# Keys of the dilated groups, and group 0's values, turned in 32x32 blocks and moved through DRAM instead of being transposed on TensorE

## The chip, the cores and the metric

The kernel runs on one core of a Trainium2 chip. The metric is the device time of one execution in microseconds (us). The runs of the kernel before took 853.75 to 854.53 us, with a median of 854.29 us.

## The reference, cut to what matters

The reference computes two layers on 512 tokens of 1024 channels, with 16 heads of 64. Layer A is the one that is changed. It projects the normalised tokens to queries, keys and values of three dilated groups (dilations 1, 4 and 16) and to a gate, and attends in each group to a window of neighbours:

```python
for g, (window, dilation) in enumerate(DILATED_PAIRS):      # (128, 1), (512, 4), (2048, 16)
    q = rms_norm(qkv[:, :, g, 0], q_gain[g])
    k = rms_norm(qkv[:, :, g, 1], k_gain[g])
    v = qkv[:, :, g, 2]
    reach = (window // 2) // dilation
    o, lse = dilated_group_attention(q, k, v, t5_bias[...], dilation, reach)
    outs.append(o)
    lses.append(lse)
alpha = jax.nn.softmax(jnp.stack(lses), axis=0)
y = jnp.sum(alpha[..., None] * jnp.stack(outs), axis=0)
y = y.reshape(b, s, BRANCH_WIDTH) * jax.nn.silu(gate)
return y @ w_out
```

Layer B, neighbourhood attention on an 8 x 64 grid, is not changed. All data are float32. A large product is made on TensorE as three products of a high and a low part (`wh`, `wl`, `hn_h`, `hn_l`).

## The kernel before, in words

**Pairs.** Layer A goes through eight pairs of heads, `hc` = 0 to 7; the text calls them the first to the eighth pair. For each pair `main_a(hc)` makes the large products: first 512 columns with the keys and values of groups 1 and 2 (`rawk`), then 512 columns with three queries and group 0's key (`rawq`), then 128 columns of group 0's values (`v0_a`), then 128 of the gate. A tile of weights is 512 columns of `wraw`; ScalarE (ACT) casts it to `wh`, VectorE (DVE) or GpSimd (POOL) subtracts to get `wl` (`split`, L127 and L131). There are four buffers of `wh` and of `wl`, and three of `wraw`, each with two tiles. A tile feeds twelve products of TensorE (PE).

**Attention beside it.** `side` yields the attention of the pair before in small pieces between the products. `scores(u)` makes the scores of half of the tokens (u = 0 and 1) into `log`, `softmax` makes `p`, and `turner` turns `p` in 32x32 blocks on DVE into `tr`, writes that to DRAM (`td`, L736) and reads it back in four parts (`pt`, L740). `weigh` multiplies `pt` with the values into `o`. Queries and group 0's key of the first six pairs are moved in the same way: `turn_q` turns `rawq`, `move_q` writes `qd` (L578) and reads `qt` (L584), and `split_q` makes `k0h`, `q0h`, `k0l`, `q0l` of it, which the next `scores` needs.

**Keys before.** `k_a(hc)` takes `rawk`, makes two sets of four 128x128 transposes on PE into PSUM (`transpose4`, tile `tp`, L210), and DVE multiplies each set with the gains into `k12` (L527). **Values before.** `v0_a` scales and permutes group 0's values into `vt` (L504), POOL copies 64 columns to its head (L505), and `v_a` makes one set of four transposes and an ACT copy into `v0` (L615).

**What sets the order.** PE's order is the order of the code. `clock` adds up a modelled time of the products; `side` goes on when `clock` has reached a due time, and `later_on(delay, job)` runs a job when `clock` has passed. Every DMA of the loop is issued by SP, in one order; an instruction there that waits holds up all behind it, the weight loads (L175) included. The order on DVE, ACT and POOL is a scheduler's, except where an instruction is kept in program order. Each pair's bias tiles `e` are read by six small DMAs (L690, L695). In the third pair `bias_rows` adds the loads and stores of `rp`, `gb_d` and `lb_d` for layer B.

Of the kernel before, what the change touches and what calls it, by code (L numbers as in the profile page):

```python
# [13 lines left out]
F32 = mybir.dt.float32  # L14
# [8 lines left out]
P = 128  # L23
# [19 lines left out]
def tile_hybrid_encoder(  # L43
# [222 lines left out]
    def squares(v, ss, i, ns):  # L266
        sq = wk.tile([P, 512], F32, tag="sq", name="sq")[:, : ns * 64]
        if len(v.shape) == 3:
            v = v.rearrange("p (a f) r -> p a f r", f=4)
            nc.gpsimd.tensor_mul(sq.rearrange("p (f a r) -> p a f r", f=4, a=4), v, v)  # L270
        else:
# [7 lines left out]
    def head_norm(raw, ss, ns, held, delay=0):  # L279


        rs = wk.tile([P, 32], F32, tag="rs", name="rs")
        rsqrt(nc.vector if ns == 8 else nc.gpsimd, rs[:, : 4 * ns], ss[:, : 4 * ns], 4 * ns, 1.0 / DH)

        def scale():
            for i in range(4):
                by = rs[:, i * ns : (i + 1) * ns].unsqueeze(2)
                if len(raw.shape) == 4:
                    v = raw[:, :, i, :].rearrange("p (h a f) r -> p f h a r", h=2, f=4)
                    by = rs[:, i * ns : (i + 1) * ns].rearrange("p (f h) -> p f h", h=2)  # L290
                    by = by.unsqueeze(3).unsqueeze(4).to_broadcast([P, 4, 2, 2, 32])
                else:
                    v = raw[:, i, : ns * 64].rearrange("p (a b) -> p a b", b=64)
                    by = by.to_broadcast([P, ns, 64])
                m = nc.vector.tensor_mul(v, v, by)
                if held or delay:
                    tc.keep_in_program_order(m)

        if held:
            later.append(scale)  # L300
        elif delay:
            later_on(delay, scale)
        else:
            scale()
# [15 lines left out]
    def trj(t):  # L320
        return t.rearrange("p (s j) -> p s j", j=4)
# [3 lines left out]

    ng = cp.tile([P, 2, KT], F32, name="ng")
    rs_n = cp.tile([P, 4], F32, name="rs_n")
    rs_trj = cp.tile([P, S], F32, name="rs_trj")
    rs_half = cp.tile([P, S], F32, name="rs_half")

    def spread():
# [38 lines left out]
    def scales_a():  # L370
        pa = spread()
        nc.scalar.mul(tjr(rs_half), to_tjr(pa), 0.5)
        nc.scalar.copy(trj(rs_trj), to_trj(pa))

    def norm(layer, k, xk):

# [45 lines left out]

    moved = lambda hc: hc < NHC - 2

    def part(n):
        return rk[:, 1024 * n : 1024 * n + 1024].rearrange("p (i c) -> p i c", i=4)

    def project_qk(n, ns, key, hc, guard, first=False, **kw):

        box = []  # L430

        def evac(i, acc):
            if not box:
                if key == "rawq":
                    t = wk.tile([P, 4 * n], F32, tag="rawq", name=key, bufs=1)
                    box.append(
                        t.rearrange("p (c i r) -> p c i r", c=16, i=4)
                        if moved(hc)
                        else t.rearrange("p (i c) -> p i c", i=4)
                    )  # L440
                elif key == "rawk":
                    box.append(part(0))
                    st["v12", hc] = part(1 + hc % 3)
# [12 lines left out]
            for dst, src in pieces:  # L456
                if first:
                    nc.scalar.copy(dst, src)
                else:
                    nc.scalar.activation(dst, src, AF.Copy, scale=rs_n[:, i : i + 1])  # L460
            if not first:
                squares(raw[:, :, i, :] if key == "rawq" and moved(hc) else raw[:, i, : ns * 64], ss, i, ns)

        tile_of = lambda hn: lambda k, i: hn[:, k, P * i : P * (i + 1)]
        yield from project(tile_of(hn_h), tile_of(hn_l), n, evac, guard, **kw)
        raw, ss = box
        if first:
            st["first"] = raw, ss
            return
        normed(raw, ss, ns, key, hc)  # L470

    def normed(raw, ss, ns, key, hc):
        head_norm(raw, ss, ns, key == "raw", 9000 if key == "rawk" and 0 < hc < NHC - 1 else 0)
        if key == "rawq" and moved(hc):
            turn_q(raw)
        st[key, hc] = raw
        stamp[key, hc] = clock[0]

    def first_out():

        raw, ss = st.pop("first")
        for i in range(4):
            for t in (raw, st["v12", 0]):
                nc.scalar.activation(t[:, i, :], t[:, i, :], AF.Copy, scale=rs_n[:, i : i + 1])
            squares(raw[:, i, :], ss, i, 4)
        normed(raw, ss, 4, "rawk", 0)

    def gate_a(hc):
# [10 lines left out]
    def v0_a(hc):  # L499
        acc = []  # L500
        yield from project_t(acc)
        yield "v", hc - 1
        vt = wk.tile([P, EXT], F32, tag="vt", name="vt", bufs=1)
        nc.vector.tensor_mul(trj(vt[:, 64:EXT]), to_trj(acc[0]), trj(rs_trj))  # L504
        nc.gpsimd.tensor_copy(vt[:, 0:64], vt[:, EXT - 64 : EXT])  # L505
        st["vt", hc] = vt
        stamp["vt", hc] = clock[0]

# [10 lines left out]
            yield from gate_a(hc)  # L519

    def k_a(hc):
        yield "wait", ("rawk", hc), 12500 if hc == 0 else 22500 if hc < NHC - 1 else 10000
        k12 = wk.tile([P, 2, 512], F32, tag="k12", name="k12", bufs=1)
        raw = st.pop(("rawk", hc))
        for g in range(2):
            tp = transpose4(raw, g * P)
            nc.vector.tensor_scalar(k12[:, g, :], tp, gk[:, g + 1 : g + 2], None, op0=ALU.mult)  # L527
# [80 lines left out]
    def v_a(hc):  # L608

        yield "wait", ("vt", hc), 2500  # L610
        vt = st.pop(("vt", hc))
        tp = bank("tp")
        for i in range(4):
            transpose(tp[:, i * P : (i + 1) * P], vt[:, i * P : (i + 1) * P])
        nc.scalar.copy(v0[hc % 2], tp.rearrange("p (i c) -> p i c", i=4))  # L615
        stamp["v", hc] = 0
        yield

# [127 lines left out]
    def attn_a(hc):  # L746
# [7 lines left out]
        def scores(u):  # L754
# [94 lines left out]
        if hc < NHC - 1:  # L849
            for u in range(2):  # L850
# [285 lines left out]
    def side():  # L1136
# [19 lines left out]
        stamp["rs", "a"] = 0  # L1156
        for hc in range(NHC):
            if hc < NHC - 1:
                yield from k_a(hc)
                yield from chain(q_a(hc), v_a(hc))  # L1160
                if moved(hc):
                    yield from st.pop(("land", hc))
                yield from attn_a(hc)
# [114 lines left out]
```

## Time and profile before

| | |
|---|---|
| median of the runs | 854.29 us |
| the profiled execution, whole | 854.65 us |
| its span, first to last instruction | 852.7 us |
| PE busy | 843.6 us (99%) |
| DVE, ACT, POOL busy | 520.2, 431.3, 307.1 us |
| DMA on SP's queue | 140.24 MB, 53.7% of 16 engines |
| TensorE clock granted | full speed in all slices of the span |

PE's busy time overlaps from one product to the next, so a busy PE may still have small gaps: they are read from the chain of waits, which lists stretches of one line with their start and length. A window's DMA share is the mean busy share of the 16 DMA engines in that stretch. A group's row gives the count, then the busy time in us and the mean length of one in ns, then the idle time ahead and what ended it.

### The profile page before, as it was taken

What the parts mean: (1) busy time and instruction counts of PE and PEld (TensorE: products, weight loads), DVE (VectorE), ACT (ScalarE), POOL (GpSimd) and SP (SyncE); (2) the same over time, 40 slices, a digit from 0 to 9 for tenths busy, and PEclk for the clock granted to TensorE, in tenths of its full rate; (3) what the DMA queues carried; (4) which work ended last, traced back from release to release, by engine and by line L of the source; (5) the groups of instructions that cost most, each with busy time, mean ns of one, the idle gap of its engine ahead of it and who ended that gap; (6) DMA issues with size and microseconds to landing.
All of it is one profiled execution on the core that took longest, in us unless ns stands there. A gap on an engine that the chain in (4) does not pass through costs nothing.

```text
span 852.7 us, 15400 instructions
## 1 busy us (share of the span) xinstructions
PE 843.6 (99%) x5547; PEld 702.7 (82%) x5547; DVE 520.2 (61%) x1335; ACT 431.3 (51%) x924; POOL 307.1 (36%) x493
## 2 busy tenths in 40 slices
PE   8999999999999999999999999999999999999998
PEld 6788878788788788788788787789998898889786
DVE  6445684674675675675675745447567656766642
ACT  7433653653652652652653554355366655665531
POOL 2252541542542542542531341121344335542411
PEclk9999999999999999999999999999999999999999
DMA  7346277477478378378375562174245654555223
GB/s 250 111 130 208 87 226 219 153 222 227 137 230 241 105 239 240 98 238 238 96 247 153 147 190 78 60 244 142 82 142 150 168 162 149 170 163 160 99 98 126
DMA packets 65372, 141.23 MB, mean 166 GB/s; under 512 B 5904, under 2 KB 23248, under 8 KB 65296
## 3 DMA queue, kind: packets, MB, share of 16 engines
q1 hardware_dynamic: 65008, 140.24, 53.7%
q8 instruction: 44, 0.72, 0.4%
q14 instruction: 32, 0.26, 0.1%
q10 hardware_dynamic: 288, 0.01, 0.0%
HBM read 109.11 MB, written 31.12 MB: 164 GB/s over the span
## 4 chain that ended last, share of the span: by engine, by line
PE 87%; ACT 4%; DMA 4%; DVE 3%; issue 1%; POOL 1%; SPq 0%; ACTq 0%; POOLq 0%; DVEq 0%
PE acc L206 74%; PE log L206 5%; PE o L206 5%; PE tp L210 3%; DMA qd<-rawq 1%; ACT p L655 1%; ACT p L814 1%; DMA rp<-in_rpb 1%; ACT p L1067 1%; DMA qt<-qd 1%; POOL sq L270 1%; ACT wh L127 1%; DMA hg<-in_head_gain 0%; DVE wl L131 0%; DMA eb<-lb_d 0%
## 5 line engine op out<-in xcount | busy, mean ns | idle before, releaser
L127 ACT CAST wh<-wraw 128x512 fp32r<-128x512 f32 (+1 forms) x276 | 162.0, 588 | 291.4 <-PE acc L206 251.0
L206 PE MATMUL acc<-wh,hn_h 128*128 128x512 f32 (+1 forms) x768 | 294.2, 383 | 1.7 <-ACT wh L127 0.9
L206 PE MATMUL acc<-wh,hn_l 128*128 128x512 f32 (+1 forms) x768 | 286.3, 373 | 0.0
L206 PE MATMUL acc<-wl,hn_h 128*128 128x512 f32 (+1 forms) x768 | 285.8, 372 | 0.4 <-DVE wl L131 0.4
L131 POOL TENSOR_TENSOR wl<-wraw,wh 128x512 fp32r<-128x512 f32 (+1 forms) x110 | 137.0, 1245 | 359.4 <-ACT wh L127 320.0
L131 DVE TENSOR_TENSOR wl<-wraw,wh 128x512 fp32r<-128x512 f32 (+1 forms) x166 | 111.1, 670 | 135.8 <-ACT wh L127 131.5
L206 PEld LDWEIGHTS acc<-wh,hn_h 128*128 128x128 f32 x768 | 144.6, 188 | 29.3 <-issue 4.9
L206 PEld LDWEIGHTS acc<-wh,hn_l 128*128 128x128 f32 x768 | 144.4, 188 | 20.8
L206 PEld LDWEIGHTS acc<-wl,hn_h 128*128 128x128 f32 x768 | 144.8, 189 | 19.8 <-DVE wl L131 0.9
L206 PE MATMUL acc<-hn_h,wh 128*128 128x512 f32 x192 | 77.0, 401 | 0.9 <-ACT rawq L460 0.6
L206 PE MATMUL acc<-hn_h,wl 128*128 128x512 f32 x192 | 74.9, 390 | 0.0
L206 PE MATMUL acc<-hn_l,wh 128*128 128x512 f32 x192 | 74.8, 390 | 0.0
L655 ACT ACTIVATE p<-p,mn 128x512 f32<-128x512 f32 (+3 forms) x128 | 69.3, 586 | 0.0
L814 ACT ACTIVATE p<-p,mn 128x512 f32<-128x512 f32 (+1 forms) x64 | 44.8, 701 | 45.0 <-DVE mn L803 44.1
L273 DVE TENSOR_REDUCE ss<-sq 128x4 f32<-128x256 f32 (+1 forms) x96 | 48.4, 504 | 30.7 <-POOL sq L272 19.7
L727 DVE STREAM_TRANSPOSE tr<-p 128x512 f32<-128x512 f32 (+1 forms) x80 | 53.7, 682 | 9.9 <-ACT p L655 9.5
L272 POOL TENSOR_TENSOR sq<-rawk 128x256 f32<-128x256 f32 x64 | 40.5, 639 | 52.7 <-ACT rawk L460 44.9
L206 PE MATMUL acc<-y_h,wh 128*128 128x512 f32 x128 | 52.1, 407 | 0.0
L206 PE MATMUL acc<-y_h,wl 128*128 128x512 f32 x128 | 50.0, 391 | 0.0
L206 PE MATMUL acc<-y_l,wh 128*128 128x512 f32 x128 | 49.9, 390 | 0.0
L206 PEld LDWEIGHTS acc<-hn_h,wh 128*128 128x128 f32 x192 | 36.1, 188 | 10.8 <-ACT rawk L460 2.1
L206 PEld LDWEIGHTS acc<-hn_h,wl 128*128 128x128 f32 x192 | 36.0, 188 | 7.7
(138 smaller groups left out, 1087.0 us busy)
## 6 DMA issues: line engine op xcount, KB each, us to landing
wraw<-in_w SPq DMA_DIRECT2D x95, 512.0 KB
wraw<-in_w SPq DMA_DIRECT2D x38, 384.0 KB
td<-tr SPq DMA_DIRECT2D x14, 1024.0 KB
pt<-td SPq DMA_DIRECT2D x56, 256.0 KB
qd<-rawq SPq DMA_DIRECT2D x6, 1024.0 KB
qt<-qd SPq DMA_DIRECT2D x24, 256.0 KB
td<-tr SPq DMA_DIRECT2D x6, 896.0 KB
pt<-td SPq DMA_DIRECT2D x24, 224.0 KB
```

The costliest lines, as they stand in the source:

```text
L127: nc.scalar.copy(h, raw)
L131: eng.tensor_sub(l, raw, h.bitcast(F32))
L206: nc.tensor.matmul(o, l, r, **kw)
L210: nc.tensor.transpose(o, i, ident)
L270: nc.gpsimd.tensor_mul(sq.rearrange("p (f a r) -> p a f r", f=4, a=4), v, v)
L272: nc.gpsimd.tensor_mul(sq, v, v)
L273: nc.vector.tensor_reduce(ss[:, i * ns : (i + 1) * ns], sq.rearrange("p (a b) -> p a b", b=64), axis=AX.X, op=ALU.add)
L655: nc.scalar.activation(pr, pr, AF.Copy, scale=mn[:, 3:4])
L727: nc.vector.transpose(dst, src[:, :n].rearrange("p (i b k) -> p i b k", b=4, k=32))
L814: nc.scalar.activation(row, row, AF.Exp, bias=mn[:, 1:2], scale=-1.0, accum_out=mn[:, 2:3])
L1067: nc.scalar.activation(pr[:, o : o + n], pr[:, o : o + n], AF.Exp, bias=mn[:, 0:1], scale=-1.0, accum_out=mn[:, 2:3])
```

## The change

The keys of the first seven pairs no longer pass PE's transposes. The evacuation of `rawk` writes them to a new layout (`rk_a`: four blocks `a` of 384 columns, of which the first 256 are the keys). After the scaling with the norm, DVE turns both groups in 32x32 blocks in place. `move_k` then writes the tile to DRAM in one DMA (`kd`) and reads it back as `k12` in four DMAs. The values of group 0 of the first six pairs are turned by DVE too, into the last 128 columns of each block, after POOL's copy; they travel with the keys of the next pair, and POOL then puts them into `v0`, doubled because they are now scaled with `rs_half` (`rs_trj` is gone). ACT multiplies `k12` with the gains in place. `attn_a` reads `k12` in four runs of 32 columns where it read 128 columns in a row. The first half's reads of `pt` are due 10500 instead of 8500 behind their write.

The place is shown on three engines. On PE, in the steady part (fifth pair), the keys' two sets of transposes stood between products of the next pair's projection (`acc` is the accumulator, `rawk` the keys); before:

```order
L206 MATMUL acc<-wh,hn_l 128x512
L210 MATMUL tp<-ident,rawk 128x128 x4
L206 MATMUL acc<-wh,hn_h 128x512
L206 MATMUL acc<-wl,hn_h 128x512
L206 MATMUL acc<-wh,hn_l 128x512
L206 MATMUL acc<-wh,hn_h 128x512
L206 MATMUL acc<-wl,hn_h 128x512
L206 MATMUL acc<-wh,hn_l 128x512
L210 MATMUL tp<-ident,rawk 128x128 x4
```

and after:

```order
L206 MATMUL acc<-wh,hn_l 128x512
L206 MATMUL acc<-wh,hn_h 128x512
L206 MATMUL acc<-wl,hn_h 128x512
L206 MATMUL acc<-wh,hn_l 128x512
L206 MATMUL acc<-wh,hn_h 128x512
L206 MATMUL acc<-wl,hn_h 128x512
L206 MATMUL acc<-wh,hn_l 128x512
L206 MATMUL acc<-wh,hn_h 128x512
```

The products follow each other without the transposes; over the program PE has 20 such sets less, 14 of keys and 6 of values.

On SP, in the third pair (`td` and `pt` are the turned scores, `rp`, `gb_d`, `lb_d` the bias of layer B, `e` the bias of the next pair), before:

```order
L736 DMA td<-tr 128x4x512
L411 DMA rp<-in_rpb 128x248
L175 DMA wraw<-in_w 128x1024
L740 DMA pt<-td 32x4x512 x2
L416 DMA gb_d<-rp 128x248
L417 DMA lb_d<-lb 128x376
L690 DMA e_2052<-l_d 128x1x256 x2
L695 DMA e_2053<-l_d 128x1x224 x4
L175 DMA wraw<-in_w 128x1024
L740 DMA pt<-td 32x4x512 x2
L736 DMA td<-tr 128x4x512
L175 DMA wraw<-in_w 128x1024
```

and after, from `lb_d` on (`k_1881` is `k12`):

```order
L424 DMA lb_d<-lb 128x376
L579 DMA kd<-rawk 128x4x384
L763 DMA e_2036<-l_d 128x1x256 x2
L768 DMA e_2037<-l_d 128x1x224 x3
L587 DMA k_1881<-kd 32x4x384 x4
L768 DMA e_2037<-l_d 128x1x224
L175 DMA wraw<-in_w 128x1024
L813 DMA pt<-td 32x4x512 x2
L809 DMA td<-tr 128x4x512
L813 DMA pt<-td 32x4x512 x3
L175 DMA wraw<-in_w 128x1024
```

The write of the keys and its four reads come in ahead of the first of these weight loads. Two reads of the first `td` that stood ahead of `gb_d` now stand behind the second `td`, and the first read of the second `td` has come ahead of the second weight load. In the other pairs the weight load behind the second `td` stands ahead of that read.

On DVE, in the fourth pair, before:

```order
L295 TENSOR_TENSOR rawk<-rawk,rs 128x256 x4
L131 TENSOR_TENSOR wl<-wraw,wh 128x512
```

and after:

```order
L301 TENSOR_TENSOR rawk<-rawk,rs 128x2x4x32 x4
L306 STREAM_TRANSPOSE rawk<-rawk 128x4x128 x2
L131 TENSOR_TENSOR wl<-wraw,wh 128x512
```

The two turns have come between the scaling and the next `wl`.

The diff, cut to its core:

```diff
@@ head_norm, scale()
+                elif len(raw.shape) == 5:
+                    v = raw[:, :, :, i, :].rearrange("p (h f) g x -> p g h f x", f=2)
+                    by = rs[:, i * ns : (i + 1) * ns].rearrange("p (g h) -> p g h", h=2)
+                    by = by.unsqueeze(3).unsqueeze(4).to_broadcast([P, 2, 2, 2, 32])
...
+            if len(raw.shape) == 5:
+                for g in range(2):
+                    tc.keep_in_program_order(nc.vector.transpose(raw[:, :, g, :, :], raw[:, :, g, :, :]))
...
@@ scales_a
-        nc.scalar.copy(trj(rs_trj), to_trj(pa))
...
+    moved_k = lambda hc: hc < NHC - 1
+    rk_a = rk[:, :1536].rearrange("p (a y) -> p a y", a=4)
...
@@ project_qk, evac
-                pieces = [(raw[:, i, :], acc[:, :256]), (st["v12", hc][:, i, :], acc[:, 256:])]
+                keys = raw[:, i, :], acc[:, :256]
+                if moved_k(hc):
+                    keys = raw[:, :, :, i, :], acc[:, :256].rearrange("p (g a x) -> p a g x", g=2, a=4)
+                pieces = [keys, (st["v12", hc][:, i, :], acc[:, 256:])]
...
@@ normed
+        if key == "rawk" and moved_k(hc):
+            move_k(hc, 17500 if hc else 4000)
...
@@ v0_a
-        nc.vector.tensor_mul(trj(vt[:, 64:EXT]), to_trj(acc[0]), trj(rs_trj))
+        in_trj = lambda t, order: t.rearrange(f"p ({order}) -> p t r j", t=4, j=4)
+        nc.vector.tensor_mul(
+            in_trj(vt[:, 64:EXT], "t r j"), in_trj(acc[0], "j t r"), in_trj(rs_half, "t j r")
+        )
         nc.gpsimd.tensor_copy(vt[:, 0:64], vt[:, EXT - 64 : EXT])
+        if moved(hc):
+            src = vt[:, :S].rearrange("p (i b x) -> p i b x", i=4, b=4)
+            dst = rk_a[:, :, 256:].rearrange("p b (i x) -> p i b x", i=4)
+            tc.keep_in_program_order(nc.vector.transpose(dst, src))
+            stamp["v", hc] = 0
+            return
...
+    def move_k(hc, delay):
+        n = 384 if hc else 256
+        d = dr.tile([4, P, 384], F32, name="kd", tag="kd", bufs=2)
+        box = []
+        def write():
+            tc.keep_in_program_order(nc.sync.dma_start(d.rearrange("a p y -> p a y")[:, :, :n], rk_a[:, :, :n]))
+            stamp["k12", hc] = 0
+        def read(a):
+            if not box:
+                box.append(wk.tile([P, 4, 384], F32, tag="k12", name="k12", bufs=1))
+            dst = box[0][32 * a : 32 * a + 32, :, :n]
+            src = d[a].rearrange("(b k) y -> k b y", b=4)[:, :, :n]
+            tc.keep_in_program_order(nc.sync.dma_start(dst, src))
+        def landed():
+            kv = box[0]
+            for g in range(2):
+                k = kv[:, :, P * g : P * g + P]
+                tc.keep_in_program_order(nc.scalar.activation(k, k, AF.Copy, scale=gk[:, g + 1 : g + 2]))
+            if hc:
+                src = kv[:, :, 256:].rearrange("p b (i x) -> p b i x", i=4)
+                dst = v0[(hc - 1) % 2].rearrange("p i (b x) -> p b i x", b=4)
+                nc.gpsimd.tensor_scalar(dst, src, 2.0, None, op0=ALU.mult)
+            st["k12", hc] = kv, st.pop(("v12", hc))
+        later_on(delay, write)
+        for n_, a in enumerate((0, 2, 1, 3)):
+            later_on(delay + 6000, partial(read, a))
+        later_on(delay + 17000, landed)
...
@@ attn_a
-                                k12[hs, g, P * j : P * j + P],
+                                sb(k12[hs], P * g + 32 * j, [[384, 4], [1, 32]]),
...
-                send = partial(turned.send, pq[:, 2048 * u : 2048 * u + 2048], 8500, 1200)
+                send = partial(turned.send, pq[:, 2048 * u : 2048 * u + 2048], 8500 if u else 10500, 1200)
...
@@ side
-                yield from k_a(hc)
-                yield from chain(q_a(hc), v_a(hc))
+                yield from q_a(hc)
                 if moved(hc):
                     yield from st.pop(("land", hc))
+                else:
+                    yield from v_a(hc)
```

More of the change, by code (lines that the diff above doesn't have):

```diff
@@ L270, in squares @@
             nc.gpsimd.tensor_mul(sq.rearrange("p (f a r) -> p a f r", f=4, a=4), v, v)
+        elif len(v.shape) == 4:
+            nc.gpsimd.tensor_mul(sq.rearrange("p (g a x) -> p a g x", g=2, a=4), v, v)
         else:
@@ L327, in tile_hybrid_encoder @@
     rs_n = cp.tile([P, 4], F32, name="rs_n")
-    rs_trj = cp.tile([P, S], F32, name="rs_trj")
     rs_half = cp.tile([P, S], F32, name="rs_half")
@@ L423, in tile_hybrid_encoder, with part @@
     moved = lambda hc: hc < NHC - 2
-    def part(n):
-        return rk[:, 1024 * n : 1024 * n + 1024].rearrange("p (i c) -> p i c", i=4)
+    moved_k = lambda hc: hc < NHC - 1
+    rk_a = rk[:, :1536].rearrange("p (a y) -> p a y", a=4)
+    def part(o):
+        return rk[:, o : o + 1024].rearrange("p (i c) -> p i c", i=4)
     def project_qk(n, ns, key, hc, guard, first=False, **kw):
@@ L441, in evac @@
                 elif key == "rawk":
-                    box.append(part(0))
-                    st["v12", hc] = part(1 + hc % 3)
+                    if moved_k(hc):
+                        box.append(rk_a[:, :, :256].rearrange("p a (g i x) -> p a g i x", g=2, i=4))
+                    else:
+                        box.append(part(0))
+                    st["v12", hc] = part(1536 + 1024 * (hc % 3))
                 else:
@@ L452, in evac @@
             elif key == "rawk":
-                pieces = [(raw[:, i, :], acc[:, :256]), (st["v12", hc][:, i, :], acc[:, 256:])]
+                keys = raw[:, i, :], acc[:, :256]
+                if moved_k(hc):
+                    keys = raw[:, :, :, i, :], acc[:, :256].rearrange("p (g a x) -> p a g x", g=2, a=4)
+                pieces = [keys, (st["v12", hc][:, i, :], acc[:, 256:])]
             else:
@@ L460, in evac @@
                     nc.scalar.activation(dst, src, AF.Copy, scale=rs_n[:, i : i + 1])
-            if not first:
-                squares(raw[:, :, i, :] if key == "rawq" and moved(hc) else raw[:, i, : ns * 64], ss, i, ns)
+            if first:
+                return
+            if key == "rawk" and moved_k(hc):
+                v = raw[:, :, :, i, :]
+            elif key == "rawq" and moved(hc):
+                v = raw[:, :, i, :]
+            else:
+                v = raw[:, i, : ns * 64]
+            squares(v, ss, i, ns)
         tile_of = lambda hn: lambda k, i: hn[:, k, P * i : P * (i + 1)]
@@ L475, in normed @@
             turn_q(raw)
+        if key == "rawk" and moved_k(hc):
+            move_k(hc, 17500 if hc else 4000)
         st[key, hc] = raw
@@ L482, in first_out @@
         for i in range(4):
-            for t in (raw, st["v12", 0]):
-                nc.scalar.activation(t[:, i, :], t[:, i, :], AF.Copy, scale=rs_n[:, i : i + 1])
-            squares(raw[:, i, :], ss, i, 4)
+            for t in (raw[:, :, :, i, :], st["v12", 0][:, i, :]):
+                nc.scalar.activation(t, t, AF.Copy, scale=rs_n[:, i : i + 1])
+            squares(raw[:, :, :, i, :], ss, i, 4)
         normed(raw, ss, 4, "rawk", 0)
@@ L503, in v0_a @@
         vt = wk.tile([P, EXT], F32, tag="vt", name="vt", bufs=1)
-        nc.vector.tensor_mul(trj(vt[:, 64:EXT]), to_trj(acc[0]), trj(rs_trj))
+        in_trj = lambda t, order: t.rearrange(f"p ({order}) -> p t r j", t=4, j=4)
+        nc.vector.tensor_mul(
+            in_trj(vt[:, 64:EXT], "t r j"), in_trj(acc[0], "j t r"), in_trj(rs_half, "t j r")
+        )
         nc.gpsimd.tensor_copy(vt[:, 0:64], vt[:, EXT - 64 : EXT])
+        if moved(hc):
[3 more added lines that the diff above has]
+            stamp["v", hc] = 0
+            return
         st["vt", hc] = vt
@@ L521, in k_a @@
     def k_a(hc):
-        yield "wait", ("rawk", hc), 12500 if hc == 0 else 22500 if hc < NHC - 1 else 10000
-        k12 = wk.tile([P, 2, 512], F32, tag="k12", name="k12", bufs=1)
+        yield "wait", ("rawk", hc), 10000
+        k12 = wk.tile([P, 4, 384], F32, tag="k12", name="k12", bufs=1)
         raw = st.pop(("rawk", hc))
@@ L526, in k_a @@
             tp = transpose4(raw, g * P)
-            nc.vector.tensor_scalar(k12[:, g, :], tp, gk[:, g + 1 : g + 2], None, op0=ALU.mult)
+            dst = k12[:, :, P * g : P * g + P].rearrange("p b (i x) -> p i b x", i=4)
+            src = tp.rearrange("p (i b x) -> p i b x", i=4, b=4)
+            nc.vector.tensor_scalar(dst, src, gk[:, g + 1 : g + 2], None, op0=ALU.mult)
             yield
@@ L614, in v_a @@
             transpose(tp[:, i * P : (i + 1) * P], vt[:, i * P : (i + 1) * P])
-        nc.scalar.copy(v0[hc % 2], tp.rearrange("p (i c) -> p i c", i=4))
+        nc.scalar.mul(v0[hc % 2], tp.rearrange("p (i c) -> p i c", i=4), 2.0)
         stamp["v", hc] = 0
@@ L1158, in side @@
             if hc < NHC - 1:
-                yield from k_a(hc)
-                yield from chain(q_a(hc), v_a(hc))
+                yield from q_a(hc)
                 if moved(hc):
                     yield from st.pop(("land", hc))
+                else:
+                    yield from v_a(hc)
                 yield from attn_a(hc)
```

## The prediction, made before the changed kernel was run

> **What bounds the kernel now.** I read the page first, then the waits of TensorE (PE), the chain of waits, the groups by form, and last windows and the timeline of the stretches where the new DMAs come in. The page's first part:
>
> ```profile
> span 852.7 us, 15400 instructions
> PE 843.6 (99%) x5547; PEld 702.7 (82%) x5547; DVE 520.2 (61%) x1335; ACT 431.3 (51%) x924; POOL 307.1 (36%) x493
> PEclk9999999999999999999999999999999999999999
> ```
>
> PE is busy 99% of the span at full clock, and no other engine is over 61%. The longest waits of PE and of its weight loads:
>
> ```profile
> PE acc L206 <- ACT rawq L460: 1.4, 2, 0.8
> PEld log L206 <- issue: 7.9, 25, 0.4
> ```
>
> PE waits for data for hardly more than 1.4 us. So the order of its instructions is the time: what leaves PE is gained, and what others do counts only where PE then waits. The chain of waits in the steady part:
>
> ```profile
> 285.37 1.58 PE acc L206 x6
> 300.68 5.00 PE acc L206 x21
> 306.12 1.39 PE acc L206 x6
> 307.94 22.48 PE acc L206 x99
> 330.86 15.01 PE acc L206 x66
> 349.49 1.58 PE acc L206 x6
> 351.07 2.00 PE log L206 x75
> ```
>
> One pair takes 349.49 - 285.37 = 64.12 us. The breaks between products are the sets of four transposes: 300.68 + 5.00 = 305.68, and the next product starts at 306.12, 0.44 us later; 307.51 to 307.94 is 0.43, and 330.42 to 330.86 is 0.44. These are the two sets of keys and the one of values.
>
> **The change part by part.** The prices, by form:
>
> ```profile
> L210 PE MATMUL tp<-ident,rawk 128*128 128x128 f32 x128 | 19.1, 272 | 0.0
> L206 PE MATMUL log<-k,qt 64*32 64x128 f32 x1024 | 18.9, 274 | 0.0
> L206 PE MATMUL o<-pt,rawk 128*64 128x128 f32 x320 | 22.4, 278 | 0.9 <-DMA eb<-lb_d 0.9
> L727 DVE STREAM_TRANSPOSE tr<-p 128x512 f32<-128x512 f32 x68 | 46.9, 702 | 9.7 <-ACT p L655 9.3
> L527 DVE TENSOR_SCALAR k<-tp,gk 128x512 f32<-128x512 f32 x16 | 11.5, 720 | 0.8 <-PE tp L210 0.8
> L615 ACT COPY v<-tp 128x512 f32<-128x512 f32 x8 | 4.7, 585 | 5.9 <-PE tp L210 5.9
> L622 ACT ACTIVATE kh<-tp,gk 128x512 fp32r<-128x512 f32 x8 | 5.5, 690 | 7.0 <-PE tp L210 7.0
> L131 POOL TENSOR_TENSOR wl<-wraw,wh 128x512 fp32r<-128x512 f32 x81 | 106.7, 1317 | 287.7 <-ACT wh L127 263.5 <-issue 9.3 <-DVE mn L1057 5.8
> ```
>
> *PE.* 14 sets of keys and 6 of values leave: 20 x 0.44 = **8.8 us gained**. A transpose's record is 272 ns long, but records overlap, so the breaks of the chain are the price.
> The page "TensorE: Matmul & The Clock Gate", section "Part 4: PE-mode transpose", of the Trainium skill gives about 275 ns for a 128x128 transpose within a kernel; the record's length agrees with it, the break does not, and by it the gain would be some 22 us.
>
> *Strided keys.* `k12` is now read in runs of 32 columns. The trace has no such score product; the nearest is `o<-pt,rawk`, whose moving operand already comes in such runs: 278 ns against 274 for the scores. I take nothing. The ends are 0.3 us (1.5% of 18.9) and, if each took twice its time, 18.9 us; the row of like reading is the nearer.
>
> *DVE.* 20 turns of 128x512 come (14.0 us at 702 ns) and 14 multiplications go (10.1 us at 720), in all 4 us more beside 332 us of idle. The turns stand ahead of a `wl` (1.4 us later) where each `wl` has four buffers; zero, from 0 to 1 us. *ACT.* 14 passes over half of `k12` (9.7 us at 690 ns) against 6 copies gone (3.5 us): 6 us more beside 421 us of idle. *POOL.* 6 moves into `v0` at about 1.3 us, 8 us beside 545. None of them is on the path; their cover is PE's products, and the keys are wanted some 30 us after they should land (due 34.5 us behind their projection by the code's clock, their scores 69 us behind it). Evacuation and scaling in other strides: zero.
>
> *DMA.* Each pair writes 128 x 4 x 384 x 4 bytes = 0.79 MB and reads as much. These go on the one queue of SP, past the weight loads, the reads of `pt`, the write of `qd` and the reads of `qt`. Rates in windows of before (PE, PEld, DVE, ACT, POOL, clock, DMA share, GB/s):
>
> ```profile
> 170.00:173.00 3.00, 3.00 (x82) 2.52 (x82) 1.82 (x8) 0.21 (x1) 0.00 (x0) 1.00 1.03 359
> 178.50:183.00 4.50, 4.50 (x24) 3.72 (x23) 4.49 (x7) 4.50 (x9) 3.00 (x4) 1.00 0.31 90
> 130.00:133.00 3.00, 3.00 (x15) 2.49 (x14) 3.00 (x6) 0.62 (x1) 0.77 (x1) 1.00 0.27 91
> 147.00:153.00 6.00, 6.00 (x28) 4.70 (x26) 2.54 (x6) 4.16 (x10) 3.14 (x6) 1.00 1.02 250
> 319.50:322.00 2.50, 2.50 (x13) 2.07 (x12) 2.43 (x4) 0.56 (x2) 1.15 (x1) 1.00 0.25 84
> 329.50:331.50 2.00, 2.00 (x13) 1.66 (x12) 0.69 (x1) 1.21 (x2) 0.00 (x0) 1.00 0.41 96
> ```
>
> The first is mostly a write: 359 GB/s, so a write of keys takes 2.2 us. The fourth is mostly reads of `qt`: 250 GB/s, so its four reads take 3.2, together **5.5 us of the queue a pair**. The ends are 4.4 us (all at 359) and 10.9 (reads at the 90 GB/s of the second window, where the small `e` loads run and 0.31 x 16 = 5 engines are busy). I stay with 250: these reads are cut like those of `qt`, over 32 partitions.
> The page "DMA: Bandwidth & Descriptors", section "Why a DMA increments its semaphore by 16 and not by 1", of the Trainium skill says that a DMA is spread over the largest number of engines up to 16 that divides the slowest dimension of both sides. For `e` (four) the busy engines agree; for the keys' 128 and 32 rows it gives 16, so the sum stands; were it four, the third pair below would pay 5 us more.
>
> *Third pair.* Here the chain of DMAs was tight. SP, ACT and POOL there, and the PE product that needs that tile:
>
> ```profile
> 183.67 1.62 SPq L736 DMA_DIRECT2D td<-tr  x1
> 186.21 0.35 SPq L175 DMA_DIRECT2D wraw<-in_w  x1
> 196.36 0.79 SPq L740 DMA_DIRECT2D pt<-td  x2
> 197.64 0.62 ACT L127 CAST wh<-wraw 128x512 fp32r<-128x512 f32 x1 [3.77 <-DMA wraw<-in_w]
> 198.34 1.31 POOL L131 TENSOR_TENSOR wl<-wraw,wh 128x512 fp32r<-128x512 f32 x1 [4.51 <-ACT wh L127]
> 204.10 0.39 PE L206 MATMUL acc<-wh,hn_h 128*128 128x512 f32 x1
> ```
>
> The second `td` lands at about 196.3, when its first read goes out. Ahead of it come 5.5 us of keys, and two reads of `pt` (0.52 MB, 2.1 us) have moved behind it: 199.7. The weight load of 186.21 now stands behind the first read of this `td`, so it goes out at some 200.5 and, with 0.79 MB ahead of its end (3.2 to 3.8 us), lets ACT cast at 204.0, 6.4 us late. What starts all this has come 2.6 us earlier (six sets in two pairs): 201.4; `wl` is ready 0.70 + 1.31 us later, at 203.4. PE gets there eight sets earlier, at 204.10 - 3.5 = 200.6. PE waits **3 us** (2.8; from 0, if reads overlap the tail, to 8, at the slow end).
>
> *Queries of the second pair.* `qt` lands late too, and the scores need what is made of it:
>
> ```profile
> 153.07 1.11 ACT L603 CAST k0h<-qt 128x512 fp32r<-128x512 f32 x1 [0.51 <-DMA qt<-qd]
> 155.20 0.75 DVE L626 SCALAR_TENSOR_TENSOR q0l<-qt,gk,q0h 128x512 fp32r<-128x512 f32 x1
> 158.28 1.59 PE log L206 x44
> 345.21 1.18 ACT L603 CAST k0h<-qt 128x512 fp32r<-128x512 f32 x1
> 347.41 0.74 DVE L626 SCALAR_TENSOR_TENSOR q0l<-qt,gk,q0h 128x512 fp32r<-128x512 f32 x1
> ```
>
> `q0l` is ready at 155.95, 2.3 us ahead of PE; PE comes another 1.3 us earlier (this pair's three sets), so 1.0 is left. Of the 5.5 us the window 130 to 133 takes 0.73 x 3 = 2.2. PE waits 5.5 - 2.2 - 1.0 = **2.3 us**, from 0 to 4.5.
>
> *Steady pairs.* `q0l` is ready at 348.15, PE at 351.07 less 1.3: 1.6 us to spare, and ACT's `k0h` at 345.21 shows no wait for `qt`, so there is more. The windows at 319.5 and 329.5 take 1.9 + 1.2 of the 5.5 us: 2.4 late. I take zero, from 0 to 0.8 in three pairs.
>
> *Sum* against the profiled execution: 854.65 - 8.8 + 2.8 + 2.3 = 850.95. The median of the runs is 0.36 us lower (854.29), so the forecast is **850.5 us**.
>
> **Rivals.** *No wait at all* (25%): DMAs fill holes and PE never sees them. For it: PE lost nothing to far fuller stretches so far (1.4 us), and four buffers of `wh` lie between a late load and PE. Against: ACT already waits 3.77 us for the load above. 854.3 - 8.8 = 845.5 us.
>
> *Queries late in every pair* (28%, the rival on the other side): `qd` stands behind all new bytes, and `qt` behind its landing. If no hole is filled the lateness is 5.5 us; less 1.6 to spare, PE loses 3.9 in each steady pair, 11.7 in three, and 2.2 more in the second: 864. It makes the kernel slower than before where the steady pairs lose over (854.3 - 850.5) / 3 = 1.3 us each, so where `qt` is over 2.9 us late. For it: the window 147 to 153 is full, at 1.02. Against: the holes of 2.5 and 2 us. Half of this chance I give to 852.6 to 856, the rest to slower, about 858 (2.5 us each).
>
> *Strided keys cost* (3%): scores at twice their time give 850.5 + 18.9 = 869; only above 20% of that does it decide. Against it is the row of `o`.
>
> *Transposes cost their full record* (4%): 80 x 0.272 = 21.8 us gained, with the waits as above 837.5 us. Against: the breaks of 0.44 us.
> This is the time by the page on TensorE named above.
>
> **How the numbers follow.** The forecast has 40%. Of 0.2% (1.7 us, about what a measurement can tell from no change): faster, below 852.6, are the forecast, no wait and full records: 0.69. Within it falls half of the late queries and a bit of the forecast's edge: 0.16. Slower are the rest and strided keys: 0.15. The range reaches from no wait, 844.8, to 856, which leaves out 4% below and 14% above; the forecast's own is 847 to 853.
>
> **What would show it.** Right: 20 sets of transposes less, a steady pair of 64.12 - 1.32 = 62.8 us, scores at the same length, ACT waiting some 6 us for a weight load in the third pair with PE waiting behind it, and `k0h` waiting for `qt` in the second. Wrong: breaks in PE's chain ahead of `log` in the fourth to sixth pairs (late queries), `log` longer than 2.00 us a half (strided keys), or PE waiting for `k12`.

## The result, and the profile after

The changed kernel took 872.25 us (median of 6 runs, 870.66 to 879.07), the kernel before 854.14 us on the same chip: ratio 1.0234, 95% interval 1.0213 to 1.0255. It is 2.3% slower, where 850.5 us were forecast. The page's first part, of the changed kernel:

```profile
span 870.9 us, 15311 instructions
PE 845.0 (97%) x5467; PEld 698.2 (80%) x5467; DVE 521.1 (60%) x1341; ACT 433.7 (50%) x931; POOL 311.9 (36%) x499
PEclk9998999998999999999999999999999999999999
```

The 80 transposes are gone (5547 to 5467 instructions of PE), and DVE, ACT and POOL have only 0.9, 2.4 and 4.8 us more to do. But PE's busy share fell from 99% to 97%, and the granted clock dips, which it did nowhere before. The waits of the changed kernel (engine, line and what it waited for; us in total, times, longest):

```profile
POOL v L597 <- DMA k<-kd: 65.5, 6, 13.4
...
ACT wh L127 <- DMA wraw<-in_w: 49.3, 13, 8.2
...
PE acc L206 <- POOL wl L131: 7.9, 3, 6.3
...
PE acc L206 <- ACT gt L522: 6.5, 4, 4.0
...
ACT k L593 <- DMA k<-kd: 6.4, 2, 4.1
```

The same for SP's queue alone:

```profile
SPq L587 <- DMA kd<-rawk: 23.4, 6, 5.7
```

Before, PE's longest entry was 1.4 us for `rawq`. Now it waits for `wl` of POOL and for the evacuation `gt` of ACT. The waits of other engines have grown too: POOL stands 65.5 us for the keys' reads, ACT waits 49.3 us for weight loads, and SP stands 23.4 us ahead of the reads until the write `kd` has landed. ACT's line in the kernel before:

```profile
ACT wh L127 <- DMA wraw<-in_w: 21.2, 7, 4.9
```

The costliest place is the third pair. POOL's timeline there (start, length, what, in brackets the idle time before it):

```profile
186.16 1.06 POOL L270 TENSOR_TENSOR sq<-rawq 128x512 f32<-128x512 f32 x1 [0.47 <-POOL wl L131]
196.83 1.49 POOL L597 TENSOR_SCALAR v<-k 128x512 f32<-128x512 f32 x1 [9.61 <-DMA k<-kd]
198.29 2.04 POOL L270 TENSOR_TENSOR sq<-rawq 128x512 f32<-128x512 f32 x2
200.28 1.27 POOL L131 TENSOR_TENSOR wl<-wraw,wh 128x512 fp32r<-128x512 f32 x1
```

And the chain of waits, there and in the steady part:

```profile
187.44 9.22 DMA k<-kd
...
201.61 28.66 PE acc L206 x115
...
233.90 1.58 PE acc L206 x6
...
320.56 3.88 DMA k<-kd
324.61 1.50 POOL v L597
326.29 1.25 POOL wl L131
327.56 10.22 DMA wraw<-in_w
339.56 23.67 PE acc L206 x96
363.23 3.62 PE o L206 x48
366.85 1.58 PE acc L206 x6
```

The last read was issued at 187.44 and landed 9.22 us later. POOL stood idle for 9.61 us at the move into `v0`, and a `wl` stood behind it in the queue. PE waited 6.3 us for that `wl`. In the steady part two pairs take 366.85 - 233.90 = 132.95 us, 66.5 each where 64.1 were before. The chain, which ran on PE alone there, now goes by the keys' reads, POOL's move, a `wl` and a weight load before it comes back to PE. What followed the wait in the third pair is seen in windows (from and to in us, length, then busy time of PE, PEld, DVE, ACT, POOL, then the granted clock, DMA share, GB/s):

```profile
196.00:199.50 3.50, 0.00 (x0) 0.00 (x0) 0.14 (x1) 1.33 (x2) 2.67 (x3) 1.00 1.02 329
200.00:206.50 6.50, 4.89 (x12) 3.83 (x13) 5.88 (x16) 1.22 (x3) 4.43 (x5) 0.50 0.49 150
207.00:210.00 3.00, 3.00 (x15) 2.49 (x14) 3.00 (x7) 1.26 (x3) 0.07 (x1) 1.00 0.99 254
```

From 200 to 206.5 the clock is 0.50, and PE's twelve products there start 0.43 us apart; from 207 the clock is 1.00 again and fifteen fit into 3 us.

### The profile page after: what moved, and what is told of

The parts are those of the page before. It is cut to its first block, busy times and chain, and to the rows that moved or that the text cites. A ratio compares the mean times of both kernels' runs of the same rounds, so it can differ in the third digit from the quotient of the medians.

```text
span 870.9 us, 15311 instructions
## 1 busy us (share of the span) xinstructions
PE 845.0 (97%) x5467; PEld 698.2 (80%) x5467; DVE 521.1 (60%) x1341; ACT 433.7 (50%) x931; POOL 311.9 (36%) x499
## 3 DMA queue, kind: packets, MB, share of 16 engines
q1 hardware_dynamic: 72736, 150.73, 57.4%
## 4 chain that ended last, share of the span: by engine, by line
PE 66%; DMA 15%; DVE 6%; ACT 5%; POOL 3%; issue 2%; SPq 2%; ACTq 0%; POOLq 0%; DVEq 0%
PE acc L206 56%; PE log L206 4%; DMA wraw<-in_w 4%; PE o L206 4%; DMA k<-kd 3%; DMA qd<-rawq 3%; PE tp L210 2%; DMA kd<-rawk 2%; DMA qt<-qd 2%; ACT p L887 1%; POOL sq L270 1%; DVE wl L131 1%; ACT p L728 1%; DMA e<-l_d 1%; SPq L587 1%
## 5 line engine op out<-in xcount | busy, mean ns | idle before, releaser
L206 PE MATMUL acc<-wh,hn_h 128*128 128x512 f32 (+1 forms) x768 | 294.6, 384 | 9.1 <-ACT gt L522 6.5
L206 PE MATMUL acc<-wl,hn_h 128*128 128x512 f32 (+1 forms) x768 | 287.1, 374 | 1.5 <-POOL wl L131 0.8
L206 PE MATMUL acc<-wh,hn_l 128*128 128x512 f32 (+1 forms) x768 | 287.0, 374 | 0.0
L206 PEld LDWEIGHTS acc<-wh,hn_h 128*128 128x128 f32 x768 | 145.3, 189 | 40.1 <-ACT gt L522 8.6
L206 PEld LDWEIGHTS acc<-wl,hn_h 128*128 128x128 f32 x768 | 145.6, 190 | 21.6 <-POOL wl L131 1.2
L206 PEld LDWEIGHTS acc<-wh,hn_l 128*128 128x128 f32 x768 | 145.2, 189 | 21.0
L206 PE MATMUL acc<-hn_h,wl 128*128 128x512 f32 x192 | 76.6, 399 | 7.2 <-POOL wl L131 7.1
L206 PE MATMUL acc<-hn_h,wh 128*128 128x512 f32 x192 | 77.6, 404 | 1.3 <-ACT rawq L479 1.1
L206 PE MATMUL acc<-hn_l,wh 128*128 128x512 f32 x192 | 75.6, 394 | 0.0
L206 PE MATMUL acc<-y_h,wh 128*128 128x512 f32 x128 | 52.1, 407 | 0.0
L206 PEld LDWEIGHTS acc<-hn_h,wl 128*128 128x128 f32 x192 | 36.6, 190 | 17.4 <-POOL wl L131 9.7
L206 PE MATMUL acc<-y_h,wl 128*128 128x512 f32 x128 | 50.0, 391 | 0.0
L206 PE MATMUL acc<-y_l,wh 128*128 128x512 f32 x128 | 49.9, 390 | 0.0
L206 PEld LDWEIGHTS acc<-hn_h,wh 128*128 128x128 f32 x192 | 36.5, 190 | 11.4 <-ACT rawk L479 2.1
L206 PEld LDWEIGHTS acc<-hn_l,wh 128*128 128x128 f32 x192 | 36.5, 190 | 7.1
```

What stands on the lines that cost most here:

```text
L206: nc.tensor.matmul(o, l, r, **kw)
```

## The experiments

Two theories stood at the start. The queue theory: the gains on ACT and the move into `v0` on POOL stand too early in queues that go in order. The transfer theory: the new bytes and SP's wait make the weight loads and the queries late, whoever reads the keys. All ratios below are to the kernel before on the same chip, with 95% intervals. The third to the sixth run leave the keys' way between partitions out of the result and serve for their times alone.

**1. The move into `v0` on ACT.**

```diff
-                nc.gpsimd.tensor_scalar(dst, src, 2.0, None, op0=ALU.mult)
+                tc.keep_in_program_order(nc.scalar.mul(dst, src, 2.0))
```

> The move of the values into v0 goes from POOL's queue to ACT's, right behind the two gains; nothing else is changed. Queue theory (the instructions that need the keys' reads stand too early in the in-order queues of POOL and ACT, and the weight tiles behind them come late): POOL no longer waits for the reads, so the waits of PE for POOL's wl go (about 8 us with the slow clock behind the longest of them), unless ACT, which now waits for the same reads, holds the casts instead: 860 to 868 us. Transfer theory (3 MB of new bytes and SP's waits make the weight loads and the queries late, whoever reads the keys): no change, 871 to 873 us.

868.85 us, 1.0171 (1.0150 to 1.0192): 0.6% less than the changed kernel's 1.0234. POOL's wait is a part, but a smaller one than the queue theory expected. (The new bytes are 10.5 MB over the program, 150.73 MB on SP's queue against 140.24, not 3.)

**2. And the three instructions later on ACT.**

```diff
-        later_on(delay + 17000, landed)
+        later_on(delay + 27000, landed)
```

> As the first, and the three instructions on ACT are due 27 instead of 17 us of the code's clock behind the write, so that they come behind the evacuation of the gate. Queue theory: no engine reaches them before the reads have landed, PE has only the waits that the DMAs make themselves, 848 to 855 us. Transfer theory: 869 to 873 us.

866.72 us, 1.0154 (1.0126 to 1.0182). The queue theory expected 848 to 855 and missed; the result is nearer to the transfer theory.

**3. Nobody reads what was moved.**

```diff
-                box.append(wk.tile([P, 4, 384], F32, tag="k12", name="k12", bufs=1))
+                box.append(spare)
...
-            kv = box[0]
+            kv = wk.tile([P, 4, 384], F32, tag="k12", name="k12", bufs=1)
...
-                nc.scalar.activation(k, k, ...)
+                nc.scalar.activation(k, rk_a[:, :, P * g : P * g + P], ...)
...
-                src = kv[:, :, 256:].rearrange(...)
+                src = rk_a[:, :, 256:].rearrange(...)
```

> The write of the keys and its four reads are made as before, but the reads go into a tile that no one uses; the gains and the move take the turned keys and values straight from the tile that the write reads, so the moving between partitions is left out of the result. All bytes and all instructions stay, only the wait for the reads is gone. Queue theory: 846 to 853 us. Transfer theory: 867 to 872 us, as the weight loads stand behind the same bytes.

864.95 us, 1.0145 (1.0111 to 1.0179). Without any wait for the reads most of the loss stays. Where it comes from is seen in the fourth pair, first in SP's timeline (the spare tile is a part of `y_l` that is not yet in use):

```profile
243.63 0.38 SPq L579 DMA_DIRECT2D kd<-rawk  x1
244.25 0.35 SPq L175 DMA_DIRECT2D wraw<-in_w  x1
247.91 2.76 SPq L587 DMA_DIRECT2D y_l<-kd  x4
250.77 0.54 SPq L763 DMA_DIRECT2D e<-l_d  x1
...
253.07 3.76 SPq L768 DMA_DIRECT2D e<-l_d  x2
256.94 1.35 SPq L175 DMA_DIRECT2D wraw<-in_w  x1
```

And in ACT's:

```profile
259.91 1.33 ACT L593 ACTIVATE k<-rawk,gk 128x512 f32<-128x512 f32 x2
267.58 1.14 ACT L127 CAST wh<-wraw 128x512 fp32r<-128x512 f32 x2 [6.33 <-DMA wraw<-in_w]
268.62 0.58 ACT L522 COPY gt<-acc 128x512 f32<-128x512 f32 x1
```

SP issues nothing from 244.6 to 247.9: it waits for the write to land. The six `e` loads come only then, and the weight loads behind them. ACT waits 6.33 us for such a load, and the evacuation `gt` stands behind that cast. PE's next projection takes all four accumulators, so it waits for `gt`: 6.4 us over this run (`PE acc L206 <- ACT gt L522: 6.4, 6, 2.3`). While the `e` loads run, the queue moves little:

```profile
252.50:260.00 7.50, 7.50 (x34) 6.22 (x34) 4.72 (x7) 4.32 (x9) 6.33 (x6) 1.00 0.35 99
```

**4. No write and no reads.** As the third, without the five `later_on` lines of `write` and `read`.

> As the third, and the write and the reads of the keys are left out. What is left of the change is PE's 20 sets less and the added work on DVE, ACT and POOL. Both theories: 845 to 848 us, the 8.8 us of the transposes gained. A third theory (the turns and gains themselves come ahead of weight tiles and make them late) would give over 852 us.

846.70 us, 0.9922 (0.9905 to 0.9938), as expected. The turns, gains and moves themselves cost some 2 us (8.8 us were to be gained, 6.7 are, by the ratio), so the third theory falls. The loss comes from the DMAs and from those who wait for them.

**5. SP doesn't wait for the write.**

```diff
-            src = d[a].rearrange(...)
+            src = st["kd"][hc - 1 if hc > 1 else hc][a].rearrange(...)
```

> As the run with the reads into a spare tile (864.95 us), but from the third pair on the reads take the tile that the pair before wrote, so SP never waits there for the write to land; the bytes and their order on the queue stay. If SP's wait (some 3.5 us a pair, with the weight loads behind it) makes the loads late: 854 to 858 us. If the bytes in the queue do it: 862 to 866 us.

856.83 us, 1.0054 (1.0035 to 1.0073): of the 864.95 us, 8 us were SP's wait. SP's wait ahead of the reads fell from 23.1 us in the third run to 8.6, as the first two pairs keep theirs.

**6. The write alone.** As the third, without the four reads.

> As the run with the spare tile, without the four reads: the write's 0.79 MB a pair stay, SP's wait for it goes. If SP's wait does it: 847 to 850 us, as without any of these DMAs (846.7). If the bytes do it: 853 to 858 us, about half of the way.

847.49 us, 0.9945 (0.9927 to 0.9963). The write costs some 2 us, give or take 2. The reads' bytes and SP's wait are both gone here, so this run doesn't tell them apart; the fifth does.

These runs make a ladder (ratios times 854 us): without DMAs -6.7; the write +2.0; the reads' bytes +9.3; SP's wait ahead of them +7.8; the engines that wait for the reads +7.6. The sum is +20.0. Each step is known to some 2 to 4 us, and the steps depend on their order.

**7. The `e` loads issued by ACT.** As the second run, with `nc.scalar.dma_start` for `nc.sync.dma_start` in `bias_a`.

> As the run with the three instructions late on ACT (866.72 us), and the six small loads of e are issued by ACT, so they run on a queue of their own and the weight loads no longer stand behind them. If the weight loads are late because the new bytes stand in one line with the slow e loads (8 to 9 us for 0.7 MB): 848 to 854 us, also faster than before (853.9). If SP's wait alone does it: 860 to 867 us.

882.90 us, 1.0361 (1.0328 to 1.0395). Neither expectation held. ACT stood still in its own issues (DMA issues are marked ACTq):

```profile
318.49 0.60 ACT L127 CAST wh<-wraw 128x512 fp32r<-128x512 f32 x1
319.00 0.72 ACT L728 ACTIVATE p<-p,mn 128x512 f32<-128x512 f32 x1
321.65 4.07 ACTq L768 DMA_DIRECT2D e<-l_d  x2
325.76 0.62 ACT L127 CAST wh<-wraw 128x512 fp32r<-128x512 f32 x1 [6.04 <-DMA k<-kd]
```

ACT is idle for 6.04 us ahead of the second cast, and PE waits for ACT's evacuations (`PE acc L206 <- ACT rawq L479: 24.8, 8, 5.5`). The profile puts the end of the idle time down to the landing of the keys' reads (`k<-kd`); what held those issues was not settled. The run says nothing on the theories, only that this is a bad place for them.
The page "DMA: Bandwidth & Descriptors" of the Trainium skill, section "Issuing engines are not separate DMA queues", says that DMAs of several engines run on the same 16 DMA engines, so that a second issuer saves only the time of the issue; the run agrees in that nothing was won, and shows that the second issuer can lose far more.

**8. Reads later.** As the second run, with `delay + 12000` for `delay + 6000` at the reads.

> As the run with the three instructions late on ACT (866.72 us), and the four reads are due 12 instead of 6 us behind the write, which puts them behind the e loads and the second td. If SP's wait does it: 853 to 859 us. If the bytes do it, wherever they stand ahead of the pair's last weight loads: 864 to 870 us.

861.65 us, 1.0117 (1.0085 to 1.0149), between the expectations. The weight loads were nearer to their time (ACT waited 56.5 us for them, 85.3 in the second run), but now the queries came late (`PE log L206 <- ACT q0h L695: 4.2, 5, 1.6`). Bytes were only moved from one waiter to another. The same run shows a stretch of ten microseconds in which the queue is idle, behind the queries' reads:

```profile
288.00:298.00 10.00, 9.37 (x105) 7.41 (x106) 7.69 (x27) 7.44 (x17) 3.26 (x2) 1.00 0.01 2
```

**9. The `e` loads in that idle stretch.** As the second run, and:

```diff
@@ move_q, read
             left[0] -= 1
+            if not left[0]:
+                later_on(4000, lambda: st.update({("e", hc + 1): bias_a(hc + 1)}))
@@ bias_a: its DMAs are kept in program order
@@ main
-            if hc:
+            if hc and not moved(hc - 1):
                 st["e", hc] = bias_a(hc)
```

> As the run with the three instructions late on ACT (866.72 us), and the six loads of e for the next pair are issued behind the reads of qt and one weight load, where the queue is idle for about 10 us in each pair (288 to 298 us in the run with late reads). They no longer stand ahead of the weight loads of the values and the gate. If the loads of weights are late because the new bytes and the wait for the write come on top of the slow e loads: 846 to 852 us. If SP's wait alone does it: 860 to 866 us.

**845.05 us, 0.9899 (0.9885 to 0.9914)**: this version beats both kernels. The keys' bytes and SP's wait are still there (26.4 us over 7 pairs), but they cost nothing now. ACT waits only 8.6 us for weight loads:

```profile
SPq L587 <- DMA kd<-rawk: 26.4, 7, 4.5
...
ACT wh L127 <- DMA wraw<-in_w: 8.6, 4, 5.0
```

The steady part of its chain of waits is free of breaks:

```profile
280.10 2.00 PE log L206 x75
282.10 9.74 PE acc L206 x42
291.84 1.98 PE log L206 x75
293.82 43.73 PE acc L206 x192
337.55 3.62 PE o L206 x48
341.17 1.58 PE acc L206 x6
342.76 2.00 PE log L206 x75
```

A pair takes 342.76 - 280.10 = 62.66 us, and between 293.82 and 337.55 no set of transposes is left.

**10. And the reads later.** Both edits of the eighth and ninth.

> As the run before it, and the reads of the keys are due 12 instead of 6 us behind the write. If both parts (SP's wait and the place of the bytes) count: 845 to 849 us, close to the 846.7 without the DMAs. If the late reads now make the queries late, as in the run with late reads alone (861.65 us, PE waited some 9 us for q0h and q0l): 850 to 856 us.

851.16 us, 0.9975 (0.9960 to 0.9989). The second expectation held in size, not quite in place (the profiled execution, 854.00 us, is the slowest of twelve): PE waited 0.9 us for `q0h` in one pair, and 4.8 us once in the seventh pair, for ACT's copy of its values (`PE log L206 <- ACT v L690: 4.8, 1, 4.8`). The 9 us that the expectation gives for the run with late reads are waits of PE's weight loads (6.4 and 2.4); its products waited 5.7 us.

**11. The kernel before with the `e` loads moved.**

> The kernel before, with the e loads moved in the same way and nothing else. PE does not wait for a weight load there, so 853 to 855 us, no change, by both theories; a gain of over 1 us would say that a part of what the two runs above win has nothing to do with the keys.

852.37 us, 0.9997 (0.9988 to 1.0006): no change. So the gain of the ninth is that of the keys and values; the room in the queue is worth something only to a kernel that needs it.

**12. Products with zeros ahead of the third pair's wait.**

```diff
+            if count[0] == 710:
+                for _ in range(24):
+                    nc.tensor.matmul(o, zero[...], zero[...], start=False, stop=False)
             nc.tensor.matmul(o, l, r, **kw)
```

> The changed kernel with 24 products with zeros (5.4 us of PE at full clock) ahead of the product at which PE waits 6.4 us in the third pair. If the half clock behind that wait (12 products at twice their time) comes of PE's standing still: the granted clock stays at 1.0 there and the third pair is 2.4 us shorter, 869 to 871 us. If it comes of something else (the rate of the transfers, say): the half clock stays, 872 to 873 us.

871.73 us, 1.0209 (1.0188 to 1.0231): in the time, too little to tell from the changed kernel. The window tells it, beside that of the changed kernel above (200 to 206.5 us):

```profile
200.00:206.50 6.50, 4.98 (x22) 4.13 (x23) 5.89 (x16) 1.10 (x2) 4.36 (x5) 1.00 0.76 237
```

POOL's `wl` came as late as before (PE's products went on at 201.52 instead of 201.61), but the clock stayed at 1.00 and 22 products fit where 12 did. The half clock came of PE's standing still. This rests on one profiled execution of each kernel; the mean granted clock of their runs, 0.994 to 0.998 with the zeros and 0.986 to 0.994 without, points the same way.

**13. The changed kernel with the `e` loads moved, and nothing else.**

> The changed kernel with the e loads moved into the idle stretch of the queue and nothing else: the gains stand where they stood on ACT, and the move into v0 on POOL. If these places cost something by themselves, as the 7.3 us between the changed kernel and the run with the spare tile say: 849 to 854 us. If they cost only because the reads were late behind the e loads: 845 to 847 us, as with both edits (845.05).

856.45 us, 1.0041 (1.0027 to 1.0055), slower than both expectations. The clock is at full speed in all slices, PE's long waits for `wl` and `gt` are gone, but POOL still stands 60.8 us for the reads, and PE waits in many small places and 2.7 us once for the values' copy in the seventh pair:

```profile
POOL v L597 <- DMA k<-kd: 60.8, 6, 13.3
...
PE log L206 <- ACT v L690: 2.7, 1, 2.7
...
PE acc L206 <- POOL wl L131: 1.4, 3, 0.7
```

With the second and the ninth this makes a square. Changed kernel: +2.3%. Queues alone: +1.5%. Transfers alone: +0.4%. Both: -1.0%. Both theories were right in part, and each edit is worth more when the other is made: 16 us for the transfers alone and 22 on top of the queues; 5.5 for the queues alone and 11 on top of the transfers, by the medians. The 6 us between these are known to some 3 or 4.

## Why the prediction was wrong

The forecast of 850.5 us missed by 21.7 us. The gain was sized rightly. What failed are two terms taken as zero (what waits behind the new instructions, and the steady pairs) and one that is missing (SP's wait between the write and the reads).

**PE's gain: right.** 8.8 us were forecast; the ninth run shows 8.2 (853.30 to 845.05), and its pair of 62.66 us meets the forecast 62.8. The transposes' full record (837.5 us) is ruled out; "no wait at all" (845.5 us) is what the ninth run made of the change.

**Strided keys: right.** The row of the scores in the changed kernel, with 274 ns as before:

```profile
L206 PE MATMUL log<-k,qt 64*32 64x128 f32 x1024 | 18.9, 274 | 0.0
```

**"None of them is on the path; their cover is PE's products": this step failed.** The work was sized well, and the fourth run has all of it at 846.70 us. What was missed is where it waits. "The keys are wanted some 30 us after they should land" is true of PE. But POOL and ACT reach the move and the gains when their queue comes to them, and whatever stands behind is wanted at once. The text had not asked what is queued behind these three instructions.

The second costliest place shows it too, and the prediction has no term for it: the first pair's keys, which are due earlier than the others (4000 behind their scaling, not 17500). ACT's timeline in the changed kernel:

```profile
65.96 0.62 ACT L127 CAST wh<-wraw 128x512 fp32r<-128x512 f32 x1 [5.73 <-DMA wraw<-in_w]
68.83 1.33 ACT L593 ACTIVATE k<-k,gk 128x512 f32<-128x512 f32 x2 [2.25 <-DMA k<-kd]
70.58 0.58 ACT L522 COPY gt<-acc 128x512 f32<-128x512 f32 x1
```

SP stood 5.7 us for the write there, ACT stood for a weight load and then for the reads, and `gt` came behind both. PE waited 4.0 us for it, up to 71.20 us, and ran at half clock behind the wait.

**"5.5 us of the queue a pair": the term was sized by bytes alone.** Its rate held: the window in which the reads of the third run go out (247.0 to 252.5 us) shows 247 GB/s against 250. (2.2 and 3.2 are 5.4, not 5.5, and the first pair moves 0.52 MB each way, not 0.79.) But the time in which SP stands between the write and its reads was not in the sum at all: 23.4 us over six pairs. In the ladder, 14.5 us less of it (23.1 to 8.6) were worth 7.8. SP's waits for the landings of `td` and `qd` fell from 69.6 to 56.5 us meanwhile, so that with `kd` it stood only 10 us longer than before; that suggests that the place of a wait counts more than its length.

**"Steady pairs: I take zero": this step failed too.** Only the queries were followed there. The last weight loads of a pair, those of the values and the gate behind the six `e` loads, were looked at in the third pair alone. In the steady pairs they came late as well. Where the prediction saw holes in the queue (the windows at 319.5 and 329.5), the hole that decides is the ten microseconds behind the queries' reads, past everything that was late. "Late queries in every pair", the rival on the other side, named the right sign; in the changed kernel the queries were a small part of it. The half of the scores that waits is longer by 1.4, 1.2 and 1.1 us in the second, fourth and sixth pair, of which the waits list shows 1.2 us for `q0h` and `q0l`.

**Third pair: 2.8 us by a late weight load.** PE lost 6.3 us there, and 2.4 more to the half clock (12 products at 0.20 us each). The wait was for POOL's `wl` behind the move into `v0`, not for the weight load, and it came 58 large products earlier than forecast, in the gate's projection (in the kernel before, these two products start at 190.47 and 204.10 us). The forecast product ran at 217.19 us without waiting. So the pair was right, the product and the mechanism were not: that PE lost time in this pair at all was luck. The reads took 9.22 us to land instead of 3.2, behind small `e` loads: the slow end of the term.

**Second pair: 2.3 us.** The half of the scores that waits took 3.40 us from its first product to its last, against 2.00 in the first pair, so PE lost 1.4, and 0.35 just ahead of it. The mechanism held, and the loss is within the range given.

**The clock** had no term, since the profile before shows full speed in all slices. Behind the waits it cost some 7 us: in the stretches that begin at 71.2, 201.6 and 339.6 us, 13, 12 and 9 products start some 0.43 us apart instead of 0.23.

**The rivals.** None had this cause. The 869 us of strided keys come nearest to 872.25, but the row of the scores rules them out, and late queries were to give 858 to 864.

## What to carry to other kernels

Where a step is moved from a busy engine to others, ask for each new instruction that waits what stands behind it in its queue, on each engine and on the DMA issuer; when its result is wanted says nothing on that. A move through DRAM costs its issuer the round trip as well as the bytes: find an idle stretch of the queue first, and put there what can go early. Then test both repairs together: here one alone left 0.4% or 1.5% of loss, and both made a gain of 1.0%.

## What was not expected of the hardware

A wait of 4.0 to 6.3 us on PE costs more than itself: in the changed kernel the granted clock was 0.50 for 5.0 to 5.6 us after it, and products with zeros in the wait kept it at 1.00. Such a stretch stands there behind a wait of 1.9 us too (339.56 us). In the run with the spare tile, waits of up to 2.3 us for `gt` left none, but waits of 1.4 and 1.1 us for `q0h` were followed by one (the clock is 0.50 from 161.9 to 165.3 and from 230.2 to 233.6 us). So the length of the wait alone doesn't tell.
The page "TensorE: Matmul & The Clock Gate" of the Trainium skill, section "Part 1: The HAM clock gate", says that the gate goes by PE's activity in free-running windows of 3.4 us. A stretch that follows a short wait at one place and not at another agrees with that, and so does the length of the stretches, 3.4 or 6.8 us here.

A run of small loads holds up what stands behind it: in the third run's window with the `e` loads the queue moved 99 GB/s at a DMA share of 0.35, and the ninth run, which takes them out of the way of the weight loads, is 21.7 us faster than the second.
